# Two output tiles of a hybrid decoder layer: their late products tile by tile, and their copies put earlier in the schedule

## The chip, the cores and the metric

The kernel is one launch on one core of a Trainium2 chip. The metric is the device time of that launch in microseconds (us). Five engines run side by side, each working off its own list of instructions in order: TensorE (PE in the profile, its weight loads PEld), VectorE (DVE), ScalarE (ACT), GpSimd (POOL) and SyncE (SP). SP and POOL here mostly issue transfers. Semaphores tie the lists together.

## The reference, cut to what matters

One decoder layer over 528 positions (16 learned ones and 512 tokens) with 1024 channels: pooling over time and a state space scan (SSD) run on the same projections, gates merge the two, an MLP follows. The change lies where the scan's result `y_ssd` is multiplied by `w_ssd_out` while the scan's last group of heads is still running.

```
u = rmsnorm(h, mix_norm_w)
proj = u @ w_in
y_pool = pool_mixer(u_pool, pool_w_group, pool_scale) @ w_pool_up
y_ssd = mamba2_branch(z, xbc, dt_raw, ...) @ w_ssd_out
h = h + (gate_pool * y_pool + gate_ssd * y_ssd) @ w_o
v = rmsnorm(h, mlp_norm_w)
h = h + relu(v @ w_ff1) ** 2 @ w_ff2
out = rmsnorm(h, final_norm_w)[:, N_META:]
```

## The kernel before

All matrix work is done in a split form: a float32 factor is kept as a high and a low part (`whi`, `wlo` for weights, `yh`, `yl` for the scan's result), and each product is three matmuls: high by high, high by low, low by high. The high part of a weight block comes from a cast on ACT, the low part from a subtraction on DVE. Both read a raw block (128 x 1024 float32, 512 KB) that SP loads. There are three raw buffers in the stretch of the change (a fourth one lives inside the scan), four `whi` and four `wlo`.

The scan goes over eight groups of heads. Each group gives two of the 16 row tiles of `y_ssd` (the list `ys`). The output `w_ssd_out` is computed for eight tiles of 128 channels, `d` from 0 to 7, in three parts over the 16 rows: rows 0 to 7 early (`out_half`), the middle part with rows 8 to 13 beside the last group's scan (`out_part`), and rows 14 and 15 after it. `out_part` (the function printed below) does the following. For `d` 0 and 1 it opens two PSUM tiles, `psp0` and `psp1`, and multiplies rows 8 to 11. Rows 12 and 13 come from group 6 and are finished late, so their products wait in a list `late`, 2 tiles x 2 rows x 3 matmuls = 12 matmuls on line 880. Then `add` copies each PSUM tile on ACT into a staging buffer (`sp`, two buffers, line 868) and issues a transfer on POOL's queue that adds it into `acc_d` in memory (line 869). For `d` 2 to 7 each tile `psp` takes all six rows at once (18 matmuls, lines 146 to 149) and is added the same way. These tiles come from a pool `psa` with two PSUM buffers: `psp2` uses the buffer of `psp0`, `psp3` that of `psp1`, and so on. After `psp6` and `psp7` the same two buffers serve `pxx`.

The weights of `out_part` are six blocks (lines 846 and 850). Then comes `pool_pair` (line 971), the projection of a pair of pooling tiles as seven products of half size. It loads two raw blocks `a1` and `a2` (line 126) and makes four operand forms, A, S, D and B, by casts on ACT (line 132: `whiA`, `whiS`, `whiD`, `whiB`) and subtractions on DVE (line 133), with sums of the raw blocks between them (lines 979 to 984: `sm`, and `a1` overwritten in place). Its products accumulate into two PSUM banks, `pxx` (`c` in the code) and `pz`; after certain products a bank is copied out (lines 1004, 1008, 1010, 1017) before the next product is added to it. Two more blocks of `w_ssd_out` follow for rows 14 and 15 (`psl`), loaded by SP (line 95) into raw buffers as they come free, cast on ACT (line 111). Their `whi` buffers are those that `whiA` and `whiS` held.

A scheduler sets the order. The program is written with generators that `weave` runs in turn, one step of `out_part` beside one step of the last group's scan; a `yield` ends a step. The scheduler then takes instructions by priority, which is a place in the written program; `tc.high_priority(n)` gives the instructions in its body the priority of a place n instructions sooner. Each engine gets a fixed list in that way, and nothing passes anything else on its engine at run time.

Of the kernel before, what the change touches and what calls it, by code (L numbers as in the profile page):

```python
# [64 lines left out]
def kernel(ctx: ExitStack, tc, xT, x, w, fx, f1, f2, vec, fnw, out):  # L65
# [21 lines left out]
    def block_tiles():  # L87
        b = nblk[0]
        nblk[0] += 1
        return (b, raw_tile(f"raw{b}"),  # L90
                wp.tile([P, 1024], F32R, tag="whi", name=f"whi{b}"),
                wp.tile([P, 1024], F32R, tag="wlo", name=f"wlo{b}"))

    def block_load(t, c):
        nc.sync.dma_start(t[1][:, c], w[t[0], :, c])
# [5 lines left out]
    def after(*ins):  # L101
        st = ExitStack()
        for i in ins:
            if i is not None:
                st.enter_context(tc.issue_after(i.ins))
        return st
# [36 lines left out]
    def mm3s(ps, pairs, first=True, last=True):  # L143

        for n, ((ah, al), (bh, bl)) in enumerate(pairs):
            pe.matmul(ps, ah, bh, start=first and n == 0, stop=False)  # L146
            pe.matmul(ps, ah, bl, start=False, stop=False)
        for n, ((ah, al), (bh, bl)) in enumerate(pairs):
            pe.matmul(ps, al, bh, start=False, stop=last and n == len(pairs) - 1)
# [43 lines left out]
    def psum2(name):  # L193
        return psa.tile([P, 1024], F32, tag="mm", name=name)

    def psum1(name):
        return psb.tile([P, 512], F32, tag="s", name=name)
# [150 lines left out]
    for t, name in ((rsh, "dgh"), (rsl, "dgl")):  # L348
        d = pre.tile([NT, 6, NT], F32R, tag="sq", name=name, bufs=2)
# [397 lines left out]
    def staged(name):  # L747
        return gtp.tile([P, SEQ], F32, tag="gt", name=name)
# [90 lines left out]
    def out_part():  # L839

        def get(n):
            t = block_tiles()
            block_load(t, slice(0, 1024))

            with after(b_meta[G - 1] if n == 1 else None):
                cast = act.copy(t[2], t[1])
            if n == 1:
                late_cast[0] = cast
            with tc.issue_after(x_decayed[G - 1].ins) if n == 1 else nullcontext():
                dve.tensor_tensor(t[3], t[1], t[2].bitcast(F32), op=ALU.subtract)  # L850
            return t

        def pieces():
            blocks = [get(0), get(1)]
            for n in range(6):
                t = blocks[n] if n < 2 else get(n)
                for j in range(NK):
                    c = slice(j * P, (j + 1) * P)
                    yield t[2][:, c], t[3][:, c]

        un = pieces()

        def part(ps, d, ks):
            mm3s(ps, [(next(un), ys[k]) for k in ks], ks[0] == 8, ks[-1] == 13)

        def add(ps, d):
            o = staged(f"sp{d}")
            act.copy(o, ps)
            nc.gpsimd.dma_start(acc_d[d], o, accum_op=ALU.add)


        ps = [psum2(f"psp{d}")[:, :SEQ] for d in range(2)]
        for d in range(2):
            part(ps[d], d, range(8, 12))
            yield
        late = [[(next(un), ys[k]) for k in (12, 13)] for d in range(2)]
        for o in ((0, 0), (1, 0), (0, 1)):
            for d in range(2):
                for n, (a, b) in enumerate(late[d]):
                    pe.matmul(ps[d], a[o[0]], b[o[1]], start=False, stop=o[1] == 1 and n == 1)  # L880
            yield
        for d in range(2):
            add(ps[d], d)
        for d in range(2, NK):
            ps = psum2(f"psp{d}")[:, :SEQ]
            part(ps, d, range(8, 14))
            add(ps, d)
            yield
# [39 lines left out]
    for g in range(G):  # L928
        nxt = group_tiles(g + 1) if g + 1 < G else None
        fill = [group_proj(g + 1, nxt, GATE_AT.get(g))] if nxt else [out_part()]  # L930
        if g == 4:
            fill = [out_half()] + fill
        weave(ssd(g, cur), fill, 2 if g == 4 else 1, weight_sums_at(SETS_AT[g], PIECES.get(g, 12)),
              [sums_of_u(g)] if g in SUMS_AT else [])
        cur = nxt
# [115 lines left out]
    for d in range(NK):  # L1051
        ps = psum1(f"psl{d}")
# [108 lines left out]
    for n, d in enumerate(MERGE):  # L1161
# [9 lines left out]
        ps = psum2(f"pup{d}")[:, :SEQ]  # L1171
# [471 lines left out]
    for t in range(4):  # L1643
        T, st = t // 2, slice((t % 2) * P, (t % 2 + 1) * P)
        n = 0
        for half in range(2):
            parts = [(0, 512)] if half == 0 or t < 3 else [(0, 256), (256, 256)]
            for a, m in parts:
                ps = p2v[t] if T == 0 and half == 0 else lastp[:, 512:] if a else (
                    lastp[:, :512] if (t, half) == (3, 0) else psum1(f"pl{t}_{half}"))  # L1650
                ps = ps[:, a : a + m]
# [180 lines left out]
```

## Time and profile before

| quantity | value |
|---|---|
| time, median of 3 runs | 1003.77 us (1003.58 to 1005.23) |
| the profiled execution, its own time | 1003.26 us |
| its span in the profile | 1001.6 us |
| between the two | 1.66 us |
| DVE busy | 804.2 us (80%) |
| ACT busy | 602.9 us (60%) |
| granted TensorE clock | 0.999 |
| transfers | 184.52 MB, mean 184 GB/s |

All profile rows of this document have times in us from the start of the span. A row of a list in order of time gives the start, the duration, the engine, the source line, the operation with what it writes and reads, and in square brackets how long the engine stood idle before it and on whom it waited. A duration covers an instruction from start to end; the next one on the same engine can start before that, so the step from row to row is the cost on a busy engine. The matmuls of 512 columns show 0.39 us each but follow each other every 0.23 us.

### The profile page before, as it was taken

Reading aid. Unit: us, or ns where it says so; the run is one execution under the profiler, and the core shown is the slowest. Engines: PE = TensorE matmul, PEld = TensorE weight load, DVE = VectorE, ACT = ScalarE, POOL = GpSimd, SP = SyncE. Lnnn points to the kernel's source line nnn. Section 1 sums busy time; section 2 is a strip of 40 time slices with the busy share of each in tenths; the row PEclk is TensorE's granted clock in tenths of the full one; section 3 lists DMA queues with packets and bytes.
Section 4 is the critical chain, followed back from the end, with each engine's and each line's share of the span. In section 5 each row is a group of like instructions: output and inputs, shape, how many; then the busy total and the mean of one; then the engine's idle time right before and its main releaser. Section 6 shows DMA issues by size and latency. Waiting matters only on the chain.

```text
span 1001.6 us, 15673 instructions
## 1 busy us (share of the span) xinstructions
PE 989.0 (99%) x6035; PEld 873.4 (87%) x6035; DVE 804.2 (80%) x1162; ACT 602.9 (60%) x855; POOL 121.9 (12%) x215
## 2 busy tenths in 40 slices
PE   9999999999999999999999999999999999999997
PEld 7889898989889999978898888888889999999986
DVE  7977997879855888978789667876988878888885
ACT  7657749494924658574345443377666666656654
POOL 0010321211212312223200001121000000000000
PEclk9999999999999999999999999999999999999999
DMA  7374868676798849678823732889354464454332
GB/s 245 89 254 140 265 182 238 195 192 199 221 262 265 232 122 278 211 161 172 286 68 127 252 101 77 259 232 323 88 197 149 142 194 138 157 185 151 129 106 84
DMA packets 61803, 184.52 MB, mean 184 GB/s; under 512 B 7072, under 2 KB 8416, under 8 KB 60704
## 3 DMA queue, kind: packets, MB, share of 16 engines
q1 hardware_dynamic: 39456, 109.00, 33.3%
q0 software_dynamic: 18240, 67.51, 26.4%
q10 hardware_dynamic: 4032, 7.00, 1.9%
q8 instruction: 47, 0.77, 0.3%
q14 instruction: 28, 0.23, 0.1%
HBM read 173.13 MB, written 58.59 MB: 231 GB/s over the span
## 4 chain that ended last, share of the span: by engine, by line
PE 84%; DVE 7%; ACT 4%; DMA 3%; issue 1%; SPq 0%; ACTq 0%; DVEq 0%
PE px L1451 8%; PE px L215 7%; PE alpha L1519 6%; PE pz L215 6%; PE px L1454 4%; PE px L218 4%; PE pgp L215 3%; PE alpha L1522 3%; PE pz L218 3%; PE pgs L215 3%; DMA raw<-in_w 2%; PE pqx L506 2%; PE py L691 2%; PE pgp L218 2%; PE pso L146 1%; PE wo_alpha L1213 1%
## 5 line engine op out<-in xcount | busy, mean ns | idle before, releaser
L113 DVE TENSOR_TENSOR wlo<-raw,whi 128x1024 fp32r<-128x1024 f32 (+2 forms) x88 | 102.2, 1171 | 45.0 <-ACT whi L111 29.7
L111 ACT CAST whi<-raw 128x1024 fp32r<-128x1024 f32 (+2 forms) x88 | 87.2, 1012 | 64.0 <-DMA raw<-in_w 15.8
L215 PE MATMUL px<-uh,whi 128*128 128x264 f32 (+1 forms) x320 | 81.1, 291 | 0.0
L218 PE MATMUL px<-ul,whi 128*128 128x264 f32 (+1 forms) x320 | 78.7, 284 | 0.0
L1226 DVE TENSOR_TENSOR ht<-ht,alpha 128x1024 f32<-128x1024 f32 x35 | 42.7, 1220 | 29.1 <-PE alpha L1519 29.1
L215 PEld LDWEIGHTS px<-uh,whi 128*128 128x128 f32 x320 | 60.5, 189 | 1.1 <-issue 0.9
L1149 ACT CAST shi<-rawf 128x1024 fp32r<-128x1024 f32 x42 | 44.2, 1053 | 28.0 <-PE alpha L1522 18.4
L218 PEld LDWEIGHTS px<-ul,whi 128*128 128x128 f32 x320 | 60.2, 188 | 0.4 <-issue 0.2
L1519 PE MATMUL alpha<-shi,hh 128*128 128x512 f32 x140 | 55.3, 395 | 0.7 <-DVE ht L1226 0.6
L1522 PE MATMUL alpha<-shi,hl 128*128 128x512 f32 x140 | 54.7, 391 | 0.0
L1150 DVE TENSOR_TENSOR slo<-rawf,shi 128x1024 fp32r<-128x1024 f32 x42 | 51.2, 1219 | 0.6 <-ACT shi L1149 0.6
L1454 PE MATMUL px<-vsl,shi 128*128 128x256 f32 x192 | 47.4, 280 | 0.0
L1451 PE MATMUL px<-vsh,shi 128*128 128x256 f32 x192 | 47.4, 281 | 0.0
L215 PE MATMUL pz<-uh,whi 128*128 128x512 f32 x112 | 43.8, 391 | 1.7 <-DVE xc L440 1.7
L218 PE MATMUL pz<-ul,whi 128*128 128x512 f32 x112 | 43.6, 390 | 0.0
L215 PE MATMUL px<-uh,wlo 128*128 128x264 f32 (+1 forms) x320 | 42.0, 283 | 0.0
L215 PEld LDWEIGHTS px<-uh,wlo 128*128 128x128 f32 x320 | 40.0, 188 | 0.0
L1519 PE MATMUL alpha<-slo,hh 128*128 128x512 f32 x140 | 37.4, 389 | 0.0
L1451 PEld LDWEIGHTS px<-vsh,shi 128*128 128x128 f32 x192 | 36.2, 188 | 0.9
L1454 PEld LDWEIGHTS px<-vsl,shi 128*128 128x128 f32 x192 | 36.1, 188 | 0.9
L1454 PE MATMUL px<-vl,shi 128*128 128x256 f32 x144 | 36.1, 283 | 0.0
L1451 PE MATMUL px<-vh,shi 128*128 128x256 f32 x144 | 36.0, 282 | 0.0
(599 smaller groups left out, 3068.3 us busy)
## 6 DMA issues: line engine op xcount, KB each, us to landing
raw<-in_w SPq DMA_DIRECT2D x96, 512.0 KB, 4.6
f_t<-in_f POOLq DMA_DIRECT2D x38, 512.0 KB, 7.5
f_s<-in_f POOLq DMA_DIRECT2D x26, 512.0 KB, 7.0
b<-in_f SPq DMA_DIRECT2D x21, 512.0 KB, 4.4
rawf<-in_f SPq DMA_DIRECT2D x36, 256.0 KB, 3.0
rawf<-f_t SPq DMA_DIRECT2D x36, 256.0 KB, 3.1
abc<-acs_d POOLq DMA_DIRECT2D x8, 1024.0 KB, 8.3
f_t<-f_t POOLq DMA_DIRECT2D x12, 512.0 KB, 6.7
```

The source lines that it names most:

```text
L111: act.copy(hi[:, c], raw[:, c])
L113: dve.tensor_tensor(lo[:, c], raw[:, c], hi[:, c].bitcast(F32), op=ALU.subtract)
L215: pe.matmul(o, wt, rhs[0][k][:, c], start=part == 0 and k == 0, stop=part == 1 and k == NK - 1)
L218: mm[0] = pe.matmul(o, wt, rhs[1][k][:, c], start=False, stop=False)
L506: at = pe.matmul(o, wk, f[k][0], start=start and not low and k == 0, stop=stop and low == 1 and k == 3, skip_group_check=True)
L1149: splits.append((act.copy(hi, src), dve.tensor_tensor(lo, src, hi.bitcast(F32), op=ALU.subtract)))
L1150: dve.tensor_tensor(lo, src, hi.bitcast(F32), op=ALU.subtract)))
L1226: added[0] = dve.tensor_tensor(o, o, src, op=op)
L1451: pe.matmul(ps, m, f[k][0], start=start and not low and k == 0, stop=stop and low == 1 and k == 3, skip_group_check=True)
L1454: pe.matmul(ps, m, f[k][1], start=False, stop=False, skip_group_check=True)
L1519: pe.matmul(ps[t], hh[:, p, seg, st], m, start=bool(first and not low and p == 0), stop=bool(last and low and p == 1), skip_group_check=True)
L1522: pe.matmul(ps[t], hl[:, p, seg, st], m, start=False, stop=False, skip_group_check=True)
```

## The change

In `out_part`, the loop over the 12 late matmuls is turned inside out: all six of tile 0, then all six of tile 1, where before each kind of matmul was done for both tiles. Each tile's copy and its transfer to `acc_d` are issued right after its own six matmuls, inside `tc.high_priority(100)`, where before both copies came after all 12. There are two steps now (two `yield`) instead of three.

```diff
         late = [[(next(un), ys[k]) for k in (12, 13)] for d in range(2)]
-        for o in ((0, 0), (1, 0), (0, 1)):
-            for d in range(2):
+        for d in range(2):
+            for o in ((0, 0), (1, 0), (0, 1)):
                 for n, (a, b) in enumerate(late[d]):
                     pe.matmul(ps[d], a[o[0]], b[o[1]], start=False, stop=o[1] == 1 and n == 1)
+            with tc.high_priority(100):
+                add(ps[d], d)
             yield
-        for d in range(2):
-            add(ps[d], d)
         for d in range(2, NK):
             ps = psum2(f"psp{d}")[:, :SEQ]
             part(ps, d, range(8, 14))
```

No instruction is added or removed on any engine. The lists differ on PE, ACT, DVE and POOL in and shortly behind the last group of the scan; SP's list is the same. In what follows a name such as `sp0` is the copy of tile 0, `whi58` the high part of weight block 58; the last number is a buffer's and differs between the two programs.

ACT at the edited place, before:

```order
L644 ACTIVATE abc7_4633<-abc7_4633 128x1024
L846 CAST whi58_4819<-raw58_4818 128x1024
L645 ACTIVATE abc7_4633<-abc7_4633 128x1024
L868 COPY sp0_4811<-psp0_4664 128x512
L868 COPY sp1_4814<-psp1_4665 128x512
```

and in the changed program:

```order
L644 ACTIVATE abc7_4633<-abc7_4633 128x1024
L868 COPY sp0_4757<-psp0_4664 128x512
L645 ACTIVATE abc7_4633<-abc7_4633 128x1024
L868 COPY sp1_4785<-psp1_4665 128x512
L846 CAST whi58_4810<-raw58_4809 128x1024
```

The two copies have moved ahead of the cast of block 58, and the first also ahead of the second activation on `abc`.

ACT some 10 instructions later, around the scaling of the last group's result (`sqg7` is its square, `qhg7` the high part of that), before:

```order
L703 ACTIVATE sqg7_4802<-yt7_4755 128x1024
L330 CAST qhg7_4805<-sqg7_4802 128x512
L712 ACT_TABLE_LOAD
L712 ACTIVATE rs7_4848<-png7_4845,eps_80 128x512
L868 COPY sp4_4911<-psp4_4886 128x512
```

and in the changed program:

```order
L703 ACTIVATE sqg7_4836<-yt7_4760 128x1024
L868 COPY sp4_4901<-psp4_4876 128x512
L330 CAST qhg7_4839<-sqg7_4836 128x512
L712 ACT_TABLE_LOAD
L712 ACTIVATE rs7_4870<-png7_4867,eps_80 128x512
```

Copy `sp4` stands ahead of the cast `qhg7` now. On PE the two sums of `qhg7` and its low part (lines 709 and 710) have moved from tile `psp4` into tile `psp5`.

ACT right behind that, through the operands of `pool_pair` (`yh7` are the casts of the last group's result), before:

```order
L868 COPY sp5_4939<-psp5_4914 128x512
L721 CAST yh7_0_4877<-yt7_4755 128x512
L721 CAST yh7_1_4882<-yt7_4755 128x512
L868 COPY sp6_4967<-psp6_4942 128x512
L132 CAST whiS3_5039<-sm3_5032 128x1024
L132 CAST whiD3_5045<-raw62_5028 128x1024
L132 CAST whiB3_5049<-raw63_5030 128x512
L868 COPY sp7_4989<-psp7_4970 128x512
L1004 COPY pu6_5053<-pxx3_5055 128x264
L111 CAST whi64_5177<-raw64_5176 128x1024
```

and in the changed program:

```order
L868 COPY sp5_4939<-psp5_4914 128x512
L868 COPY sp6_4967<-psp6_4942 128x512
L721 CAST yh7_0_4905<-yt7_4760 128x512
L721 CAST yh7_1_4910<-yt7_4760 128x512
L132 CAST whiS3_5039<-sm3_5032 128x1024
L868 COPY sp7_4989<-psp7_4970 128x512
L132 CAST whiD3_5045<-raw62_5028 128x1024
L132 CAST whiB3_5049<-raw63_5030 128x512
L111 CAST whi64_5177<-raw64_5176 128x1024
L1004 COPY pu6_5053<-pxx3_5055 128x264
```

Copy `sp6` stands ahead of both `yh7` casts, `sp7` ahead of `whiD` and `whiB`, and the cast of block 64 ahead of the copy on line 1004. On DVE only one pair of neighbours is exchanged (lines 113 and 1006, behind `wloB`). On POOL the transfers of the copies stand a few places earlier among the loads of `acc_d` (line 1043) and the sums of later weights.

## The prediction

> **What bounds the kernel now.** I read the page first: PE is busy for all but 12.6 us of its span, so time is won only by shortening a wait of PE, and lost as soon as PE waits somewhere new.
>
> ```profile
> span 1001.6 us, 15673 instructions
> ...
> PE 989.0 (99%) x6035; PEld 873.4 (87%) x6035; DVE 804.2 (80%) x1162; ACT 602.9 (60%) x855; POOL 121.9 (12%) x215
> ```
>
> The list of PE's waits, over the whole span, says which ones there are:
>
> ```profile
> PE psp L146 <- ACT sp L868: 1.4, 1, 1.4
> ...
> PE pz L998 <- ACT pu L1010: 0.4, 1, 0.4
> PE pxx L998 <- ACT pu L1008: 0.3, 1, 0.3
> ```
>
> The first belongs to the edited place, the second lies 38 us behind it, in the first `pool_pair`. In order of time the first looks so on PE:
>
> ```profile
> 443.53 1.09 PE L880 MATMUL psp<-yl,whi 128*128 128x512 f32 x4
> 446.06 0.50 PE L146 MATMUL psp<-yh,whi 128*128 128x512 f32 x1 [1.44 <-ACT sp L868]
> ```
>
> The 12 late matmuls end at 444.62, and the first of `psp2` starts only when copy `sp0` has emptied its PSUM buffer. ACT in the same microseconds:
>
> ```profile
> 442.58 1.06 ACT L644 ACTIVATE abc<-abc 128x1024 f32<-128x1024 f32 x1
> 443.54 1.04 ACT L846 CAST whi<-raw 128x1024 fp32r<-128x1024 f32 x1
> 444.49 1.05 ACT L645 ACTIVATE abc<-abc 128x1024 f32<-128x1024 f32 x1
> 445.44 1.05 ACT L868 COPY sp<-psp 128x512 f32<-128x512 f32 x2
> ```
>
> ACT is full there: the copy is late because a cast and an activation of 0.95 us each (row to row) stand ahead of it.
>
> **The change part by part.** *The first wait.* Tile 0's six matmuls now come first, so it is complete some 1.3 us before 444.62. Its copy follows the activation of line 644 and starts at 443.54, where the cast starts now; two copies take 1.05, so one ends some 0.59 after its start, at 444.13. PE issues its twelfth late matmul and is ready for `psp2` at about 444.4 (443.53 plus four steps of 0.23). The wait is gone: `psp2` starts at 444.4 instead of 446.06, a gain of 1.7 us. The casts pushed back by this (blocks 58 to 61) are needed by PE only after eight matmuls of `psp2` and the scan's products; two copies of together 1.05 delay them by no more than that, so this costs nothing.
>
> *Copy `sp4` ahead of `qhg7`.* ACT now stands until `psp4` is done.
>
> ```profile
> 461.53 0.62 ACT L330 CAST qhg<-sqg 128x512 fp32r<-128x512 f32 x1 [0.76 <-DVE sqg L704]
> ...
> 468.52 1.28 ACT L721 CAST yh<-yt 128x512 fp32r<-128x512 f32 x2
> 471.97 0.59 ACT L868 COPY sp<-psp 128x512 f32<-128x512 f32 x1 [2.17 <-PE psp L149]
> 472.46 1.05 ACT L132 CAST whiS<-sm 128x1024 fp32r<-128x1024 f32 x1
> 473.41 1.05 ACT L132 CAST whiD<-raw 128x1024 fp32r<-128x1024 f32 x1
> 474.65 0.63 ACT L132 CAST whiB<-raw 128x512 fp32r<-128x512 f32 x1 [0.19 <-PE psp L147]
> 476.05 0.59 ACT L868 COPY sp<-psp 128x512 f32<-128x512 f32 x1 [0.78 <-PE psp L149]
> ...
> 478.43 1.05 ACT L111 CAST whi<-raw 128x1024 fp32r<-128x1024 f32 x1 [0.58 <-PE py L1001]
> ...
> 482.28 1.05 ACT L111 CAST whi<-raw 128x1024 fp32r<-128x1024 f32 x1 [1.52 <-DMA raw<-in_w]
> 483.23 0.37 ACT L1010 COPY pu<-pz 128x264 f32<-128x264 f32 x1
> ```
>
> Before, the last matmul of `psp4` is this one on PE:
>
> ```profile
> 463.32 0.39 PE L149 MATMUL psp<-yh,wlo 128*128 128x512 f32 x1
> ```
>
> It ends at 463.71, so with the gain at 462.0 at the latest, and `qhg7` after 0.5 of copy at 462.5: at most 1.0 late. That puts the scaled result at most 1.0 late, 469.5 for the first `yh7` cast. The next item holds that cast longer, so this one costs nothing more; its cover gone, it would be worth up to 1.0.
>
> *Copy `sp6` ahead of `yh7`.* This is the edit's price. `sp6` waited for PE at 471.97; PE being 1.7 sooner, it runs at 470.27. The `yh7` casts, which ran at 468.52, come behind it, at 470.76 (0.49 for a copy, row to row): 2.2 late. DVE's list is unchanged there, and it works strictly behind them:
>
> ```profile
> 467.73 1.41 DVE L718 SCALAR_TENSOR_TENSOR yt<-yt,vs,rs 128x512 f32<-128x512 f32 x2
> 469.18 1.35 DVE L722 TENSOR_TENSOR yl<-yt,yh 128x512 fp32r<-128x512 f32 x2
> ...
> 471.16 0.69 DVE L981 TENSOR_TENSOR sm<-sm,raw 128x512 f32<-128x512 f32 x1
> ...
> 472.37 0.68 DVE L984 TENSOR_TENSOR raw<-raw,sm 128x512 f32<-128x512 f32 x1
> ...
> 474.68 1.22 DVE L133 TENSOR_TENSOR wloD<-raw,whiD 128x1024 fp32r<-128x1024 f32 x1
> ```
>
> `sm`, ready at 471.85, is ready at 474.1, so `whiS` runs at 474.1 (1.7 late). `sp7`, which now stands ahead of `whiD`, is ready at 474.35 but comes behind `whiS`, at 475.1. The overwritten `a1` (473.05 before) is there at 475.3. So `whiD` runs at 475.6 instead of 473.41, ends at 476.6, and `wloD` runs at 476.7: 2.0 late. That step frees a raw buffer for SP's load of block 65:
>
> ```profile
> 475.93 6.25 DMA raw<-in_w
> ```
>
> The load is issued at 477.9 instead of 475.93, and PE's own products are waiting for it by way of ACT: the cast of block 65 (482.28) stands ahead of the copy of `pz` (line 1010, 483.23), and the second product on `pz` must wait for that copy.
>
> ```profile
> 478.11 0.28 PE L1001 MATMUL py<-ul,whiA 128*128 128x264 f32 x1
> 478.23 0.64 PE L998 MATMUL py<-uh,wloA 128*128 128x264 f32 x4
> 478.71 0.28 PE L998 MATMUL pxx<-t0h,whiS 128*128 128x264 f32 x1
> ...
> 483.66 0.39 PE L998 MATMUL pz<-t1h,whiB 128*128 128x264 f32 x1 [0.40 <-ACT pu L1010]
> ```
>
> *Block 64's cast ahead of line 1004.* It needs `whiA`'s buffer, free after the last line-1001 matmul on `py`: 478.39 before, 476.7 now. ACT comes to it behind `whiB` at 477.0 and to line 1004 at 478.0, done 478.4. PE, which could start the S product at 477.0 (478.71 less 1.7), waits for it until 478.4. So 1.4 of the 1.7 are given back, 0.3 are left, and PE is ready for the second product on `pz` at 483.26 less 0.3, or 482.95.
>
> *The load's duration* is the unknown price. The same load took 6.25, and the loads of this size around it and behind it took, as medians over 440 to 500 and 500 to 800:
>
> ```profile
> raw<-in_w SPq DMA_DIRECT2D x10, 512.0 KB, 6.4
> ```
>
> ```profile
> raw<-in_w SPq DMA_DIRECT2D x28, 512.0 KB, 4.4
> ```
>
> The extremes of SP's loads on line 95 from 440 to 500 are these:
>
> ```profile
> DMA to landing us min/median/max: 3.5/6.7/8.9
> ```
>
> So 3.5 bounds it below and 8.9 above. I take 6.25: the same POOL transfers (three or four loads of `acc_d` and the sum of `sp7`) are in flight beside it, since their issue moves with the copies. Then it lands at 484.2, the cast runs at 484.3, line 1010 at 485.2, and the second product on `pz` starts at 485.65 (483.66 less 482.28 is 1.38 behind the cast): **2.0 us later than before**. The Trainium skill (page "DMA: Bandwidth & Descriptors", section "Queues, rings and completion order") says that each DMA engine serves in turn the queues that have work for it, a packet at a time. With that page's fit of 2.0 us and 436 GB/s, at half the rate, 512 KB would land in an estimated 4.4 us. That agrees with the row from 500 to 800 and not with the 6.25; by it the sum would be +0.2.
>
> Behind `pz` everything follows PE. Blocks 66 and 67 land behind block 65, DVE's sums of `psl` and ACT's casts move by the same 2.0. PE has no wait of over 0.6 us left to absorb it.
>
> *Sum:* −1.7 (first wait) +1.4 (S product) +2.3 (second product on `pz`, over its old 0.4) = +2.0. The profiled execution took 1003.26 (its span and 1.66 around it), so its like takes 1005.3. The median of the three runs is 0.51 above that execution, so I forecast 1005.8 for the median.
>
> **The rivals.**
> 1. *The load lands at the kernel's ordinary speed.* At 4.4 us it lands at 482.3 and the product starts 0.15 late: 1003.9. For it: the median of the 28 later loads. Against it: the 6.4 of the ten loads in this very stretch.
> 2. *Part of the gain stays (not slower).* If the load lands in under 3.55 us (482.95 less the 1.48 from landing to product, less 477.9), PE is there first and keeps the 0.3 and the old wait's 0.4: 1003.1. If, besides, `sp6` and block 64's cast hold nothing up, all 1.7 stays: 1002.1. Only the fastest load of the stretch, 3.5, reaches this point.
> 3. *The load fares like its neighbour.* The slowest of these loads, 8.9, is that of block 66, issued right behind block 65's. At that price block 65 lands 2.65 later: 1008.4. It decides from about 7.5 us on.
> 4. *The change does not do what it says.* `sp0` may find its staging buffer taken until 445.4, when it was seen to start; then PE gains nothing, `sp6` stays at 471.97, and `yh7`, `wloD` and the load are 1.7 later still: 1007.5. Nothing in ACT's row at 445.44 shows a wait for a buffer, which speaks against it.
>
> The Trainium skill ("PSUM — Partial Sum Buffer", section "Engine vs sequencer instructions") states that ScalarE's queue is strictly first in, first out. By that rule `yh7` cannot pass `sp6` and the sum is the +2.0 above; if it could pass, the `pz` loss and most of the S wait would vanish, and the time would be rival 2's 1002.1. The row at 483.23, a copy that starts only as the cast ahead of it gets out, agrees with the rule.
>
> **How the numbers follow.** Forecast 0.58, rival 1 0.18, rival 2 0.07, rival 3 0.12, rival 4 0.05. The forecast's own range, with the load at 5.5 to 7 us, is 1005.0 to 1006.6. The range for 8 in 10 reaches down to 1003.2, which takes in rival 1, and up to 1008.0, short of rival 3's full price. No change is taken as within 0.2% (1001.76 to 1005.78), about what a measurement of this kernel can tell. Of the forecast 0.33 lies above that and 0.25 inside; with rivals 3 and 4 slower has 0.50. Faster, below 1001.76, needs all of rival 2 and more: 0.03. Within 0.2% is left with 0.47.
>
> **What the profile will show.** Right: no wait of PE before `psp2`, which starts near 444.4; `yh7` directly behind `sp6` at about 470.8; PE waiting about 1.4 for line 1004 before the S product and about 2.7 for line 1010; the load of block 65 issued near 477.9; the rest of the list shifted by 2. Wrong: `psp2` still waiting for `sp0`; `wloD` before 476; a load of block 65 under 5 us, which would make the price vanish; or a new wait of PE further back, in the pairs after 500, where I found none.

## The result, and the profile after

| quantity | before | after |
|---|---|---|
| median of 5 runs side by side | 1003.58 us (1002.24 to 1005.23) | 1008.01 us (1006.99 to 1008.22) |
| ratio of the times, 95% interval | | 1.0045, 1.0034 to 1.0056 |
| the profiled execution | 1003.26 us | 1007.54 us |
| its span | 1001.6 us | 1005.8 us |
| granted clock over the span | 0.999 | 0.996 |

The change makes the kernel 4.4 us slower; 2.0 were forecast, and the range ended just below what was measured. The page of the changed kernel has 2.2 us more of PE's busy time for the same number of instructions, and one slice of the clock is no longer full:

```profile
PE 991.2 (99%) x6035; PEld 876.4 (87%) x6035; DVE 803.6 (80%) x1162; ACT 602.1 (60%) x855; POOL 119.7 (12%) x215
...
PEclk9999999999999999999899999999999999999999
```

PE's waits over the span say where (engine, line, the releaser; us in total, times, the longest). The wait for `sp` is gone, and the same product on `pz` that used to wait 0.4 waits ten times that:

```profile
PE pz L998 <- ACT pu L1010: 4.1, 1, 4.1
```

The two places on PE in order of time, first `psp2` with no wait, then the S product and the second product on `pz`:

```profile
443.99 0.39 PE L146 MATMUL psp<-yh,whi 128*128 128x512 f32 x1
...
477.86 0.39 PE L998 MATMUL pxx<-t0h,whiS 128*128 128x264 f32 x1 [1.18 <-ACT pu L1004]
...
486.59 0.59 PE L998 MATMUL pz<-t1h,whiB 128*128 128x264 f32 x1 [4.08 <-ACT pu L1010]
486.98 0.42 PE L1001 MATMUL pz<-t1l,whiB 128*128 128x264 f32 x1
487.20 0.42 PE L998 MATMUL pz<-t1h,whiB 128*128 128x264 f32 x1
...
491.96 0.40 PE L146 MATMUL psl<-yh,whi 128*128 128x512 f32 x1
```

The rows behind the long wait hold the second surprise: a matmul of 264 columns takes 0.42 and follows the last by 0.22. Before, behind the product at 483.66, they took 0.29 and followed each other by some 0.12:

```profile
483.88 0.29 PE L1001 MATMUL pz<-t1l,whiB 128*128 128x264 f32 x1
484.01 0.29 PE L998 MATMUL pz<-t1h,whiB 128*128 128x264 f32 x1
...
486.68 0.39 PE L146 MATMUL psl<-yh,whi 128*128 128x512 f32 x1
```

The windows of the changed kernel in that stretch (stretch and length; busy time and instructions of each engine; then granted clock, DMA share, GB/s) say why:

```profile
484.00:486.00 2.00, 0.00 (x0) 0.00 (x0) 0.00 (x0) 0.78 (x1) 1.07 (x2) 0.76 1.02 399
486.00:488.00 2.00, 1.41 (x6) 1.41 (x7) 1.56 (x2) 0.54 (x2) 0.00 (x0) 0.50 1.03 408
488.00:490.00 2.00, 2.00 (x11) 2.00 (x10) 0.36 (x1) 1.05 (x1) 0.00 (x0) 0.50 1.02 385
490.00:492.00 2.00, 2.00 (x12) 2.00 (x11) 1.90 (x4) 0.60 (x1) 0.00 (x0) 0.53 1.02 391
```

The clock is granted at half for 6.84 us (0.76 in a stretch of 2 us is 0.96 us at half, then 4.00, then 1.88). It starts at 485.04, while PE still waits, and the 24 matmuls of `pz` and `pxx` fall into the rest of it: 5.37 us from 486.59 to 491.96, against 3.02 before (483.66 to the first `psl` product at 486.68).

The chain of waits that leads into the `pz` product is the one that was forecast, step for step:

```profile
469.78 0.59 ACT sp L868
470.37 0.53 ACT yh L721
...
475.01 1.07 ACT whiD L132
476.10 1.24 DVE wloD L133
477.35 7.77 DMA raw<-in_w
485.22 1.04 ACT whi L111
486.26 0.29 ACT pu L1010
486.59 0.59 PE pz L998
```

To add up, the same matmul is compared in both profiles at three places: ahead of the edit, in the second pair of pooling tiles, and in the MLP. Before:

```profile
405.64 0.28 PE L509 MATMUL pqx<-ul,whip 128*128 128x264 f32 x1
...
510.10 0.29 PE L998 MATMUL pz<-t1h,whiS 128*128 128x264 f32 x1
...
726.91 0.47 PE L1519 MATMUL alpha<-shi,hh 128*128 128x512 f32 x1 [0.55 <-DVE ht L1226]
...
749.04 0.39 PE L1522 MATMUL alpha<-shi,hl 128*128 128x512 f32 x1
```

After:

```profile
405.18 0.28 PE L509 MATMUL pqx<-ul,whip 128*128 128x264 f32 x1
...
515.40 0.29 PE L998 MATMUL pz<-t1h,whiS 128*128 128x264 f32 x1
...
753.33 0.39 PE L1522 MATMUL alpha<-shi,hl 128*128 128x512 f32 x1
```

The changed kernel's execution was 0.46 ahead before it reached the edit (chance: it stems from the first 20 us, where the two programs are the same), 5.30 behind at 510 and 4.29 behind at 749. So the edited stretch costs 5.76, and 1.0 comes back near 727, where PE used to wait 0.55 and waits no more.

That 1.0 is not lateness that a wait took up. Before, the chain of waits into the row at 726.91 goes back to a load of a weight block:

```profile
676.02 11.68 DMA raw<-in_w
...
687.78 1.05 ACT whi L111
```

The same cast in the changed kernel:

```profile
691.46 1.05 ACT L111 CAST whi<-raw 128x1024 fp32r<-128x1024 f32 x1 [1.04 <-DMA raw<-in_w]
```

Its load was issued 5.2 later, at 681.23, but took 10.15, 1.5 less, so ACT and DVE are only 3.7 late from there on. Over all profiles of this document, the wait near 727 is there where this load took 11.56 or more (0.2 to 1.3) and absent where it took 10.88 or less, whether PE came early or late. What makes the load shorter or longer isn't shown.

### The profile page after: what moved, and what is told of

It is laid out like the page before. It is cut to its first block, busy times and chain, and to the rows that moved or that the text cites. A ratio compares the mean times of both kernels' runs of the same rounds, so it can differ in the third digit from the quotient of the medians.

```text
span 1005.8 us, 15670 instructions
## 1 busy us (share of the span) xinstructions
PE 991.2 (99%) x6035; PEld 876.4 (87%) x6035; DVE 803.6 (80%) x1162; ACT 602.1 (60%) x855; POOL 119.7 (12%) x215
## 4 chain that ended last, share of the span: by engine, by line
PE 91%; DVE 4%; ACT 3%; DMA 1%; issue 1%; ACTq 0%; DVEq 0%
PE px L1451 8%; PE px L215 7%; PE alpha L1519 6%; PE pz L215 6%; PE px L1454 4%; PE px L218 4%; PE alpha L1522 3%; PE pgp L215 3%; PE pz L218 3%; PE pgs L215 3%; PE pqx L506 2%; PE py L691 2%; PE pgp L218 2%; PE pso L146 1%; PE wo_alpha L1213 1%; PE pf L147 1%
```

## The experiments

The scheduler's lists alone settle one question. Turn the loop over the late products and leave `high_priority` out, or keep a third step: all five engines get the changed program's lists, entry for entry. The turned loop does it all. Priority without the turned loop gives other lists; that is run 4.

All ratios below are to the kernel before, run beside each experiment on the same chip. In the rows shown, lines of the experiments' kernels are up to two higher than in the kernels above where their edits add lines. A time is a median of several executions (one alone in runs 9 and 10), and each profile is of one of them.

**1. Cast of block 64 behind the copy of line 1004.**

```diff
-        act.copy(r1[:, one], c)
+        first[p] = act.copy(r1[:, one], c)
...
-    un = units()
+    un = units([(None, first[3])])
```

> The changed kernel with one order more: the cast of block 64 (and by the scheduler's own choice then that of block 65) on ACT stands behind the copies of lines 1004 and 1010, which PE waits for; sp6 and sp7 stay ahead of yh7 and whiD. Theory (the loss arises only where a copy that PE needs stands behind a cast that waits for a load): no wait of 1.2 us at the S product, none of 4.1 us at pz, no clock below 1.00 there, although the load of block 65 is still issued near 477.4 and takes 6 to 8 us. The gain of 1.6 us before psp2 stays and the old wait of 0.4 us at pz goes: 2.0 us faster than before, some 1001.6 us. Rival (the late yh7 chain itself, through the operands S, D and B or the sums on DVE, holds PE): a wait of PE remains between 476 and 500 and the time stays above before's 1003.6 us.

Measured: 1004.75 us, ratio 1.0019 (1.0006 to 1.0032), so slower than before, where the theory had it faster. The cast of block 65 moved behind the copy of `pz` as well, since the scheduler now took that copy first. PE's waits between 476 and 500 changed place:

```profile
PE psl L147 <- DVE acc L1056: 3.3, 2, 1.7
```

The wait at `pz` is gone and that at the S product is down to 0.23, although the load of block 65 again took 7.77. But DVE's list has the low half of block 65 ahead of its sums, so DVE stood for the load instead of ACT:

```profile
486.27 1.23 DVE L113 TENSOR_TENSOR wlo<-raw,whi 128x1024 fp32r<-128x1024 f32 x1 [4.18 <-ACT whi L111]
```

The order of ACT's list is the cause of the `pz` wait. Setting it there alone moves the wait to the next list.

**2. PE kept busy in the gap.** Ten matmuls into the unused half of `pxx`'s PSUM tile, ahead of the second product on `pz`; their result is never read. (The priority of the block loads and casts also goes from 100 to 110, to keep the other lists as they were.)

```diff
+        if p == POOL_ORDER[0]:
+            with tc.issue_after(last[p].ins):
+                for n in range(10):
+                    last[p] = pe.matmul(bank[:, 512:], ones_r, uh[0][:, NM:], start=n == 0, stop=n == 9)
```

> The changed kernel with ten added matmuls of 512 columns, into an unused PSUM bank, between the product that ends at 482.5 and the pz product that waits until 486.6; every other list is as in the changed kernel, and the result is not touched. They take 10 x 0.23 = 2.3 us of the 4.1 us wait. Theory (the granted clock fell to 0.50 because PE stood idle for 4.1 us): the wait shrinks to about 1.8 us, the pz product starts at the same time, the clock stays at 1.00, and the 24 matmuls behind the wait take 3.0 us and not 5.4: 2.3 us faster than the changed kernel, 2.1 us slower than before, about 1005.7 us. Rival (the clock falls for another reason, or the matmuls of pz are slow for another): the time stays at 4.4 us above before, 1008.0 us, or more if the added matmuls cost time.

Measured: 1006.31 us, ratio 1.0035 (1.0022 to 1.0048). On PE:

```profile
482.12 2.50 PE L1016 MATMUL pxx<-uh,ones_r 128*128 128x512 f32 x10
...
485.16 0.39 PE L999 MATMUL pz<-t1h,whiB 128*128 128x264 f32 x1 [0.54 <-ACT pu L1011]
```

The product on `pz` still comes 2.9 us behind the last useful matmul, more than the wait of 2.48 that brings the half clock in run 4, yet its matmuls take 0.39 and 0.28 as before, and the windows have the clock at 1.00 throughout. So the half clock comes from PE's idle time. That rests on the trace. The load of block 65 took 6.55 in this run, with the same lists on SP and POOL, so part of the 2.1 us of span that this run is shorter by is the load's. And by the ratios the run is only 0.1% faster than the changed kernel, with overlapping intervals, where 2.3 us were forecast.

**3. POOL's loads of `m` held until block 65 is cast.**

```diff
+            held = pool.tensor_copy(seen, whi_of[1][:, :1].bitcast(F32))
...
-                with tc.issue_after(mixed[0].ins):
+                with tc.issue_after(held.ins):
```

> The changed kernel with one added copy of one column on POOL that waits for the cast of block 65; the seven loads of line 1077 stand behind it and so cannot run beside the load of block 65. Theory (that load took 7.8 us and not 6.25 because five of the line 1077 loads now run beside it, released early by the earlier sum of sp7): it takes 6.3 us or less, the wait at pz is at most 2.6 us, the clock stays at 1.00: 1.5 us plus 2.3 us less than the changed kernel, some of it given back at the wait near 727 us: 1004.2 to 1005.2 us. Rival (the load is slow because of blocks 66 and 67, issued right behind it on the same queue): it still takes 7.5 us or more and the time stays near 1008 us.

Measured: 1008.17 us, ratio 1.0044 (1.0031 to 1.0058). The load took 7.78 and the `pz` wait was 4.1, and the clock was at half for 6.8 again. These loads alone are not what stretches it.

**4. Priority without the turned loop.** The late products stay interleaved; the copies keep `high_priority(100)`.

> The kernel before with only half of the edit: the late products stay interleaved, the two copies get the priority of a place 100 instructions sooner. In ACT's list they now stand ahead of the activation of line 645 but behind the cast of block 58; yh7 stays ahead of sp6, the cast of block 64 behind line 1004. Theory (what is won before psp2 is eaten at pz, where PE waits for the load of block 65, as long as that load is not issued sooner): psp2 starts about 1 us sooner, the wait at pz grows from 0.4 to about 1.4 us, and the time is within 0.5 us of before, 1003.1 to 1004.1 us. Rival (the gain before psp2 reaches the end): 1 us faster, 1002.6 us. Rival (delaying line 645 costs the scan): a new wait before 460 and slower than 1004.6 us.

Measured: 1005.31 us, ratio 1.0026 (1.0015 to 1.0037), so slower, not the same. The wait ahead of `psp2` shrank to 0.5, but the load took 7.16 here and the wait at `pz` grew to 2.48:

```profile
484.28 0.39 PE L999 MATMUL pz<-t1h,whiB 128*128 128x264 f32 x1 [2.48 <-ACT pu L1011]
```

Behind it the clock went to half as well, and not at once:

```profile
484.00:486.00 2.00, 1.72 (x12) 1.72 (x13) 1.55 (x2) 0.23 (x1) 0.00 (x0) 0.87 1.04 397
486.00:488.00 2.00, 2.00 (x11) 2.00 (x11) 1.54 (x3) 1.05 (x1) 0.39 (x1) 0.50 1.03 408
488.00:490.00 2.00, 2.00 (x10) 1.79 (x10) 1.70 (x3) 1.13 (x2) 1.73 (x4) 0.78 0.94 318
```

0.52, 2.00 and 0.88 make 3.40 us at half clock.

**5. Nothing that PE needs up to `psl4` behind the load.** Casts of blocks 64 and 65 behind the copies on `pxx` and `pz`, the low half of block 65 behind DVE's second sum.

```diff
-    un = units()
+    un = units(lambda n: ((None, first[3]), [*psl_add[1:2], copied[3]])[n] if n < 2 else ())
```

> The changed kernel, with three places of the order set: ACT's cast of block 64 behind the copy of pxx, its cast of block 65 behind the copy of pz, and DVE's low half of block 65 behind the second sum of psl. Nothing that PE waits for before psl4 then stands behind the load of block 65. Theory (the gain ahead of psp2 is real, and only the work that stands behind the load gives it back): waits of PE at the S product and at pz under 0.3, the clock 1.00 throughout, no wait at psl4, PE 1.7 to 2.1 sooner than before at the first psl product and at 510, and the time 1.5 to 2.1 shorter than before, ratio 0.998 to 0.9985. Rival A (the place after 720, where PE already waited 0.55 for ACT's alpha, is bound by work that does not move with PE): the same lead at 510, but the wait at alpha grows to 2 and more, and the time is that of before, ratio 1.000. Rival B (DVE cannot do its sums in time in this order either, as when only the cast of block 64 was moved): a wait of PE of over 1 between psl4 and 500, ratio 1.001 or more.

Measured: 1005.65 us, ratio 1.0032 (1.0020 to 1.0044): slower than before, no gain. The first half of the theory held (no wait of over 0.5 up to `psl4`), and then came one more place:

```profile
493.92 0.74 PE L149 MATMUL psl<-yh,wlo 128*128 128x512 f32 x2 [3.02 <-DVE wlo L113]
```

The chain of waits into it, below, goes through the copy that closes `pxx` (line 1018 here, 1017 before). It stands behind the casts of blocks 66 and 67 on ACT's list and starts at 491.02; in run 8, where it stands ahead of them, it starts at 484.77.

```profile
479.50 10.50 DMA raw<-in_w
...
490.07 1.05 ACT whi L111
491.12 0.28 ACT pu L1018
```

DVE's running sums over that tile, its second sum of `psl` and the low half of block 65 all follow that copy. The clock was at half for 3.40 us again. This is rival B's wait, though not by rival B's mechanism: DVE stood 3.73 us for ACT's copy; it was not short of time.

**6. The same two casts' rule in the kernel before.**

> The kernel before, with ACT's cast of block 65 behind the copy of pz and DVE's low half of block 65 behind the second sum of psl (block 64's cast is behind the copy of pxx there already). The tiles' late products stay interleaved. Theory: the wait of 1.6 ahead of psp2 stays, the 0.40 at pz goes; 0 to 0.4 shorter than before, ratio 0.9995 to 1.000, so that the turned products are what the 1.7 to 2.1 of the run beside it come from. Rival (the gain beside it comes from the order of casts alone): this run is as much shorter than before as that one.

Measured: 1002.25 us, ratio 0.9995 (0.9986 to 1.0004). The wait ahead of `psp2` stayed (1.46), the one at `pz` went; no measurable difference, as the theory had it.

**7. POOL's last four loads of `acc_d`, and the loads of `m`, held until block 65 is cast.**

```diff
-    for d in range(NK):
+    for d in range(4):
         t_load = nc.gpsimd.dma_start(acc[d], acc_d[d])
...
+        if d == 4:
+            held = pool.tensor_copy(seen, whi_of[1][:, :1].bitcast(F32))
+            for e in range(4, NK):
+                with tc.issue_after(held.ins):
+                    nc.gpsimd.dma_start(acc[e], acc_d[e])
```

> The changed kernel, with POOL's last four loads of acc_d, and the loads of m behind them, issued only once ACT has cast block 65 (a copy of one column on POOL waits for the cast). Nothing of POOL's but sp7's transfer is then in flight beside the load of block 65. Theory (these loads share the engines with block 65 and make its 7.8): it lands in 4.0 to 5.5, the wait at pz is 0.5 to 1.8, the clock stays at 1.00 or nearly, and the time is 1.5 to 3 shorter than the changed kernel's, ratio 1.001 to 1.003. Rival (the length is of the queue of block 65 itself, or of sp7's transfer): 7 to 8 as it was, the wait at pz 3.3 to 4.3, the clock at 0.50 behind it, ratio 1.004 to 1.006. Either way the held loads land by about 492, in time for the fifth sum of psl at 495.

Measured: 1004.00 us, ratio 1.0013 (1.0003 to 1.0023). In the profiled execution the load took 7.85, the wait at `pz` was 4.2, and the clock was at half for 3.40 instead of 6.84, which makes the 24 matmuls 0.8 shorter. That is the rival's case. But at 1006.46 it is the slowest of the twelve executions, while the median ratio lies within the theory's 1.001 to 1.003. One piece of 3.40 us at half takes 0.0017 off the mean clock, so an execution with a mean of 0.999 or more had none: that is so in seven of the twelve here, and in none of the changed kernel's five or of run 3's seven. So in most executions the wait was probably short, as the theory has it. No profile of such an execution was taken, so the theory is neither confirmed nor refuted.

**8. All four copies of the pair ahead of the casts of blocks 65, 66 and 67.** Run 5, with the cast of block 65 behind the last copy of `pxx`, and DVE's low halves of blocks 66 and 67 behind its fourth sum.

```diff
-        act.copy(r1[:, two], c)
+        ended[p] = act.copy(r1[:, two], c)
...
-    un = units()
+    un = units(lambda n: ((None, first[3]), [*psl_add[1:2], ended[3]])[n] if n < 2 else ())
...
-    wgb = block(psl_add[2])
+    wgb = block(psl_add[3])
```

> The changed kernel, with ACT's cast of block 64 behind the first copy of pxx, its cast of block 65 behind the last copy of pxx (so all four copies of the pair run ahead of the casts of blocks 65, 66 and 67), DVE's low half of block 65 behind the second sum of psl and its low halves of blocks 66 and 67 behind the fourth. Theory (the gain ahead of psp2 is real; what gives it back is only that work PE needs stands behind a load on ACT or DVE, one place after the other): waits at the S product and at pz under 0.6, no wait of over 0.5 at psl, the clock 1.00 throughout, PE 1.5 to 2.0 sooner than in before at 510 (the runs' own offset at entry taken off), and the time 1.0 to 2.0 shorter than before, ratio 0.998 to 0.999. Rival A (the place after 720, where PE already waited 0.55 for ACT's alpha, is bound by work that does not move with PE): the lead at 510 is there, the wait at alpha grows by as much, ratio 0.9995 to 1.000. Rival B (with the gain DVE is the bound from 483 on, whatever the order): psl waits for DVE's sums or low halves by 1 or more, no lead at 510, ratio 1.000 or more.

Measured: 999.92 us, ratio 0.9974 (0.9963 to 0.9984): **faster than both kernels**. PE's waits have none left between the edit and 500 that is over 0.3:

```profile
PE alpha L1520 <- DVE ht L1227: 0.8, 1, 0.8
PE pxx L999 <- ACT pu L1009: 0.3, 1, 0.3
```

On ACT, the two copies run as soon as PE is done, and only then does ACT stand for the load, which took 7.69 and costs nothing:

```profile
480.41 0.38 ACT L1011 COPY pu<-pz 128x264 f32<-128x264 f32 x1 [1.08 <-PE pz L999]
484.77 0.38 ACT L1018 COPY pu<-pxx 128x264 f32<-128x264 f32 x1 [3.98 <-PE pxx L999]
485.38 1.05 ACT L111 CAST whi<-raw 128x1024 fp32r<-128x1024 f32 x1 [0.23 <-DMA raw<-in_w]
```

The same matmuls as above stand at

```profile
405.47 0.28 PE L509 MATMUL pqx<-ul,whip 128*128 128x264 f32 x1
...
508.00 0.29 PE L999 MATMUL pz<-t1h,whiS 128*128 128x264 f32 x1
...
747.15 0.39 PE L1523 MATMUL alpha<-shi,hl 128*128 128x512 f32 x1
```

0.17 ahead of before, then 2.10, then 1.89. So 1.93 are won at 510, as the theory had it, and 0.21 is lost again near 727, where the load named with the result took 11.97. It is not, as rival A has it, work that does not move with PE: ACT's cast behind that load came 1.9 sooner than before. The median is 2.7 below the kernel before's, more than the profiles' 1.7 and than the 1.0 to 2.0 that were forecast; the profiled execution is one of the two slowest of its eight.

**9. SP's loads of blocks 66 and 67 held until block 65 is cast.**

```diff
+            with after(load_behind):
+                block_load(t, slice(0, 1024))
...
+    held = nc.sync.dma_start(seen_d, whi_of[1][:, :1].bitcast(F32))
-    wgb = block(psl_add[2])
+    wgb = block(psl_add[2], None, held)
```

> The changed kernel, with SP's loads of blocks 66 and 67 issued only once ACT has cast block 65 (SP sends one column of that cast to a scratch tensor first, and waits for it; ACT's last copy of pxx comes ahead of the cast of block 66). Those two loads are late then, and the time is of no interest; the question is the load of block 65. Theory (it is stretched to 7.8 by the loads of blocks 66 and 67, issued 0.6 and 1.7 behind it on the same queue; before they came 0.9 and 4.8 behind it): 4.5 to 6.0, the wait at pz 0.8 to 2.3. Rival (it is sp7's transfer, or what POOL moves): 7 to 8, the wait at pz 3.3 to 4.1, as it was.

Measured, in one execution: the load took 7.35, the wait at `pz` 3.7, as the rival had it.

**10. Both kinds held.**

> The changed kernel, with POOL's last four loads of acc_d and its loads of m, and SP's loads of blocks 66 and 67, all issued only once ACT has cast block 65. With either kind held alone the load of block 65 took 7.85 and 7.35; the other kind was still in flight beside it each time. Those loads are late here and the time is of no interest. Theory (the engines are shared, and either kind alone is enough to fill them): with both away it takes 4.0 to 5.5, the wait at pz is 0.3 to 1.8. Rival (sp7's transfer and the four loads of acc_d issued before 474 are what holds it up, or the load has this length by itself in this place): 6.5 to 8, the wait at pz 3 to 4.

Measured, in the chain of waits: with `m` and the last `acc_d` loads held (run 7), with blocks 66 and 67 held (run 9), with both held (run 10), a row of each:

```profile
476.86 7.85 DMA raw<-in_w
```

```profile
477.17 7.35 DMA raw<-in_w
```

```profile
477.60 4.53 DMA raw<-in_w
```

The wait at `pz` was 0.8 in run 10. With the transfer of `sp7` still beside it, the load takes 4.53 when both kinds are held, and over 7 us in the two profiles with one kind held. This is one execution each, run 7's its slowest, and between executions with the same lists on SP and POOL the load varied from 6.55 (run 2) to 7.77. So that the neighbours stretch the load is likely; how much each kind does is not shown.

**11. The order of run 8 in the kernel before.**

> The kernel before (late products interleaved, no priority), with the order that made the changed kernel 0.26% faster: ACT's cast of block 65 behind the last copy of pxx, DVE's low half of block 65 behind the second sum of psl and those of blocks 66 and 67 behind the fourth. Theory (that gain is the turned products' 1.7 ahead of psp2, kept): the wait of 1.5 ahead of psp2 stays, the 0.40 at pz goes, 0 to 0.6 shorter than before, ratio 0.9993 to 1.000. Rival (the order of casts and copies alone makes the gain): ratio 0.997 to 0.998, PE 1.5 or more sooner at 510 with the wait ahead of psp2 still there.

Measured: 1001.65 us, ratio 0.9989 (0.9978 to 1.0000). The wait ahead of `psp2` stays (1.44), and PE is 0.66 sooner at 510 and 0.30 at 749, each less its 0.43 at entry. So by the profiles the order alone makes 0.30 of run 8's 1.72 us, and the rest is the turned products'. The timed ratio, just below the theory's 0.9993, allows the order alone up to 0.22% and can't rule out none; its interval and run 8's overlap slightly.

## Why the prediction was wrong

Its places and their order were right. All times below have the 0.46 of the start added, so that they compare with the kernel before.

- *First wait gone, `psp2` at 444.4, gain 1.7.* 444.45; gain 1.6. Right.
- *Copy `sp4` ahead of `qhg7` costs nothing.* No wait of PE came of it. Right.
- *Copy `sp6` ahead of `yh7`, 470.76; `wloD` 476.7; the load of block 65 issued 477.9.* 470.72, 476.56 and 477.81. Right to 0.15, through six instructions on two engines.
- *The S product gives back 1.4.* 1.2. Right.
- *The load takes 6.25 as before.* **This step failed.** 7.77. The reason given, that the same transfers are in flight beside it, was not worked out. Before, block 66 came 0.9 behind block 65 and block 67 4.8 behind; after, 0.6 and 1.7. POOL's transfers shifted too. Run 10, with both kinds held, had a load of 4.53, so its price hangs on what else is under way; which neighbour made the 1.5 stays open. Rival 3 named a slower load, and its "from about 7.5 us on" was reached. With the load of block 65 so much later, the second product on `pz` starts 3.4 later than before where 2.0 was forecast, and waits 4.08 where 2.7 was named: +1.4.
- *"Behind `pz` everything follows PE", the rest shifted by 2.* **This step failed too.** A term was missing: PE, idle for 4.08, is clocked at half for 6.84, and 24 matmuls take 2.35 longer. Run 2 shows the cause by taking it away: a gap of 2.9, filled with matmuls, leaves the clock at 1.00. And not everything followed PE: one load near 680 took 1.5 less than before, so that DVE came sooner, the 0.55 wait near 727 went, and 1.0 came back.

In sum: 2.0 forecast, +1.4 for the load, +2.35 for the clock, −1.0 near 727 makes 4.75, less the 0.46 of the start 4.3; the profiled executions differ by 4.28, the medians by 4.43. That the median of 1008.01 lies so near rival 3's 1008.4 is luck: rival 3 had a load of 8.9 and no term for the clock, and with the 7.77 measured its sum would be 1007.3. The forecast's rule for ACT, that no entry passes another, held in every row shown; the Trainium skill ("PSUM — Partial Sum Buffer", section "Engine vs sequencer instructions") states it, and the row at 484.77 of run 8, a copy that starts 6.2 us sooner than in run 5 (491.02) with its place in the list ahead of the casts, agrees. The prediction's estimate of 4.4 us from a fit of the Trainium skill ("DMA: Bandwidth & Descriptors") was no guide here: the page gives that fit for transfers issued by GpSimd (section "Anatomy of one DMA — SWDGE (gpsimd) path"), this one is SP's, and it measured 7.77.

The last-named sign of error, a new wait of PE in the pairs after 500, did not come in the changed kernel. In runs 1 and 5 new waits came one list further on, still ahead of 500.

What stays open: how long the load took in run 7's faster executions, and what decides whether it takes 6.6 or 7.8 under the same lists.

## What to carry to other kernels

When an early wait is removed, follow every in-order list that the freed time runs into up to its next load: the gain is lost at the first entry that PE needs and that stands behind a cast waiting for a transfer. Cure all such places together; here two orders that cured some of them were slower than before and the third, with all, was 0.26% faster. A wait of PE of about 2.5 us or more has a second price, the stretch at half clock behind it, and belongs in the sum as a term of its own. Before a theory is dropped on one profile, look where that execution lies among the timed ones.

## What the runs showed of the hardware

The half clock comes in whole pieces. It lasted 3.4 us behind waits of 2.48 (run 4), 3.02 (run 5), 3.7 (run 9) and 4.2 (run 7), and 6.8 behind the 4.08 of the changed kernel, the 4.09 of run 3 and a wait of 4.3 on `psl` in run 10: one piece or two, for nearly the same wait. Which of the two goes by where it sets in. In runs 4, 5, 7 and 9 that is 0.8 to 1.2 us after PE has started again, and there is one piece. In the changed kernel and in runs 3 and 10 it is 1.1 to 1.6 us before, so PE still waits in the first piece, and a second follows. The rows of run 5 where it begins and ends, in the windows:

```profile
494.00:496.00 2.00, 2.00 (x7) 1.56 (x8) 2.00 (x3) 0.00 (x0) 0.00 (x0) 0.71 0.49 106
496.00:498.00 2.00, 2.00 (x6) 1.57 (x5) 2.00 (x4) 0.24 (x1) 0.00 (x0) 0.50 0.68 195
498.00:500.00 2.00, 2.00 (x10) 1.59 (x8) 2.00 (x4) 0.81 (x1) 0.00 (x0) 0.94 0.93 305
```

The Trainium skill ("TensorE: Matmul & The Clock Gate", section "What's actually happening") states that the clock is set by PE's activity in free-running windows of about 3.4 us and falls to half after an idle one. The pieces of 3.4 us and the late start agree with such windows. That a wait of 2.48 was enough, with PE at work for 1.2 of the last 3.4 ahead of the drop in run 4, is less than the whole idle window that it names; here the measurement decides.

The waits of 1.18 at the S product and of 0.54 at `pz` in run 2 left the clock at 1.00, and so did the two of 1.61 and 1.67 at `psl` in run 1. Where between these and 2.48 the limit lies is not shown by these waits.
